# The second MLP product of a decoder layer as 2x2 block products with seven multiplications

## The chip, the cores and the metric

The kernel runs on one core of one Trainium2 chip. The metric is the device time of one execution in microseconds (us). A core has five engines with a queue each: PE (matrix products, with its weight loads shown apart as PEld), DVE (VectorE), ACT (ScalarE), POOL (GpSimd) and SP (SyncE, which here only issues DMAs). Each engine works its own queue in order and waits on semaphores for the others.

## The reference

One layer over x of 512 tokens by 1024 features, all in float32. The change touches only the last lines of it, and the residual ahead of them:

```python
merged = jax.nn.sigmoid(gate_attn) * attn + jax.nn.sigmoid(gate_conv) * conv
x = x + merged @ w_out[l]                                   # (512,1024) @ (1024,1024)

hmid = jnp.square(jax.nn.relu(rms_norm(x, norm_mlp_g[l]) @ w_ff1[l]))   # (512,1024) @ (1024,4096)
x = x + hmid @ w_ff2[l]                                     # (512,4096) @ (4096,1024)
```

Ahead of it stand the input projection, sliding-window attention over 16 heads, and a convolution of width 31 with a layer norm.

## The kernel before

**Products in three passes.** A float32 operand is split in two: a high part (a copy cast to fp32r, on ACT) and a low part (the operand minus its high part). A product takes three matmuls: high by high, high by low, low by high. `split` (lines 138 to 142) does this for a piece of weights of 128x1024: line 140 casts on ACT, line 141 subtracts on the engine it is given, POOL by default. `stationary_tiles` (from line 144) loads columns of a matrix in two DMAs of 512 KB and yields tiles for `mm_T` (lines 171 to 176), where the weights are the stationary operand. `moving_pieces` (from line 156) loads rows for `mm_M` (lines 178 to 182), where the weights are the moving operand of 512 columns. Raw weights have two buffers (tag "raw"), high and low parts three each (tags "wh", "wl").

**The order.** The code is written in the order of the computation, but a planner in the framework decides each engine's order from a cost model, with source order as priority, and gives out the buffers of a tag as they come free. Only a section at the start is ordered by hand (`manual_schedule`).

**Ahead of the MLP.** `residual` adds the w_out product to x (line 736) and squares it for the norm (738). The first 512 columns of w_out go through `moving_pieces`; the second half has its own loop (from line 750), which casts (757) and subtracts on POOL (758) in eight tiles of 128x512. `x2_norm` makes the norm of a token block with a short chain of small DVE instructions (lines 110 to 115, 133, 763) and two multiplications (767); `x2_trans` transposes it on PE and splits it into x2Th and x2Tl (192, 193).

**The MLP.** It runs in two halves (`fh`) over the 4096 hidden features. A half first makes 16 tiles of 128 hidden features by 512 tokens: 24 matmuls each (lines 174 to 176) and `ff1_evac` out of PSUM (Relu on ACT, 786; square on DVE, 787; high part on ACT, 788; low part on DVE, 789). The very first three tiles are done in two halves of 256 tokens (`EARLY`), since the last token blocks are still being normalized. Then, for each of two halves of 512 output columns, `mm_rows` multiplies them with w_ff2: 16 blocks of 128 hidden features, 4 token blocks, 3 passes (lines 180 to 182), into four PSUM banks; the sums are added to x1 on DVE (818), and in the second half stored (820). Tiles named `ps_f` in the trace are the PSUM banks of both products, `wh_f` and `wl_f` the weights' parts, `hmh` and `hml` the parts of the hidden features. Six PSUM banks (tag "mm") are shared by all of it.

Of the kernel before, what the change touches and what calls it, by code (L numbers as in the profile page):

```python
# [51 lines left out]
def tile_hybrid_block(  # L52
# [104 lines left out]
    def moving_pieces(w, r0, nk, c0, width, name, lo_eng=None):  # L157

        kk = 1024 // width
        for ch in range(nk // (2 * kk)):  # L160
            raw = wp.tile([P, 2 * kk, width], F32, name=f"rawm_{name}_{ch}", tag="raw", bufs=2)
            for j in range(2):
                r = r0 + (ch * 2 + j) * kk * P
                nc.sync.dma_start(
                    raw[:, j * kk:(j + 1) * kk, :],
                    w[r:r + kk * P, c0:c0 + width].rearrange("(k p) c -> p k c", p=P),
                )
            for j in range(2):
                yield split(raw[:, j * kk:(j + 1) * kk, :], [P, kk, width], f"{name}_{ch}_{j}", lo_eng or ge)
# [8 lines left out]
    def mm_M(ps, ah, al, wh, wl, first, last):  # L178

        pe.matmul(ps, ah, wh, start=first, stop=False)  # L180
        pe.matmul(ps, ah, wl, start=False, stop=False)  # L181
        pe.matmul(ps, al, wh, start=False, stop=last)  # L182

    def transpose_split(ps_pool, src, dst_h, dst_l, t, tag, pt="tr"):

        for half in range(2):
            tp = ps_pool.tile([P, 4, P], F32, name=f"tp_{tag}_{half}", tag=pt)
            for j in range(4):
                k = half * 4 + j
                pe.transpose(tp[:, j, :], src[half][:, j * P:(j + 1) * P], ident)  # L190
            hs = dst_h[:, half * 4:half * 4 + 4, t * P:(t + 1) * P]
            se.copy(hs, tp)  # L192
            ve.tensor_tensor(out=dst_l[:, half * 4:half * 4 + 4, t * P:(t + 1) * P],  # L193
                             in0=tp, in1=hs.bitcast(F32), op=ALU.subtract)
# [5 lines left out]
    aux = ctx.enter_context(tc.tile_pool(name="aux", bufs=2, space=PSUM))  # L200
# [70 lines left out]
    us = {}  # L271
# [421 lines left out]
    for m, (wh, wl) in enumerate(stationary_tiles(w_conv_out, 0, KD, "wc")):  # L693
        ps = psp.tile([P, S], F32, name=f"ps_co_{m}", tag="mm")
# [18 lines left out]
    x2Th = ff.tile([P, KD, S], F32R, name="x2Th")  # L713
    x2Tl = ff.tile([P, KD, S], F32R, name="x2Tl")

    def mm_rows(accs, pieces, ah, al, kk, n_major):

        n = len(pieces)
        for i in range(n - n_major):
            for j in range(kk):  # L720
                for t in range(NT):
                    k = i * kk + j
                    mm_M(accs[t], ah(k, t), al(k, t), pieces[i][0][:, j, :], pieces[i][1][:, j, :], k == 0,
                         k == n * kk - 1)
        for t in range(NT):
            for i in range(n - n_major, n):
                for j in range(kk):
# [6 lines left out]
    def residual(t, half, acc):  # L734
        cols = slice(half * S, half * S + S)
        ve.tensor_tensor(out=x1[t][:, cols], in0=x1[t][:, cols], in1=acc, op=ALU.add)
        sq = ff.tile([P, S], F32, name=f"fsq_{half}{t}", tag="tmp", bufs=5)
        se.activation(sq, x1[t][:, cols], AF.Square, accum_out=ssm[:, t, half:half + 1])
# [12 lines left out]
    pieces = []
    for i in range(NT):
        raw = wp.tile([P, 2, S], F32, name=f"raw_wout1_{i}", tag="raw", bufs=2)
        nc.sync.dma_start(raw, w_out[i * 256:(i + 1) * 256, S:D].rearrange("(k p) c -> p k c", p=P))
        for j in range(2):
            wh, wl = [ff.tile([P, S], F32R, name=f"wout1_{i}{j}{n}", tag="hm", bufs=DFF // P) for n in "hl"]
            se.copy(wh, raw[:, j, :])
            ge.tensor_tensor(out=wl, in0=raw[:, j, :], in1=wh.bitcast(F32), op=ALU.subtract)
            pieces.append((wh, wl))
# [24 lines left out]
    def ff1_evac(ps, hmh, hml, m):
        r = ff.tile([P, S], F32, name=f"r_{m}", tag="tmp", bufs=5)
        se.activation(r, ps, AF.Relu)  # L786
        ve.scalar_tensor_tensor(out=r, in0=ps, scalar=0.0, in1=r, op0=ALU.max, op1=ALU.mult)  # L787
        se.copy(hmh, r)  # L788
        ve.tensor_tensor(out=hml, in0=r, in1=hmh.bitcast(F32), op=ALU.subtract)  # L789

    NH = DFF // P // 2
    for fh in range(2):
        hmh = [ff.tile([P, S], F32R, name=f"hmh{fh}_{m}", tag="hm", bufs=2 * NH) for m in range(NH)]
        hml = [ff.tile([P, S], F32R, name=f"hml{fh}_{m}", tag="hm", bufs=2 * NH) for m in range(NH)]
        early = []
        for m, (wh, wl) in enumerate(stationary_tiles(w_ff1, fh * NH * P, NH, f"f1{fh}")):
            ps = psp.tile([P, S], F32, name=f"ps_f1{fh}_{m}", tag="mm")
            if fh == 0 and m < EARLY:
                mm_T(ps[:, 0:256], wh, wl, x2Th, x2Tl, slice(0, 256))
                early.append((ps, wh, wl))  # L800
                if m < 2:
                    x2_trans(2 + m)
                if m == EARLY - 1:
                    for i, (ps_, wh_, wl_) in enumerate(early):
                        mm_T(ps_[:, 256:512], wh_, wl_, x2Th, x2Tl, slice(256, 512))
                        ff1_evac(ps_, hmh[i], hml[i], i)
            else:
                mm_T(ps, wh, wl, x2Th, x2Tl)
                ff1_evac(ps, hmh[m], hml[m], m)
        for half in range(2):  # L810
            cols = slice(half * S, half * S + S)
            accs = [psp.tile([P, S], F32, name=f"ps_f2{fh}{half}_{t}", tag="mm") for t in range(NT)]
            pieces = list(moving_pieces(w_ff2, fh * NH * P, NH, half * S, S, f"f2{fh}{half}"))
            mm_rows(accs, pieces,
                    lambda k, t: hmh[k][:, t * P:(t + 1) * P], lambda k, t: hml[k][:, t * P:(t + 1) * P],
                    2, 2 if fh and half else 0)
            for t in range(NT):
                ve.tensor_tensor(out=x1[t][:, cols], in0=x1[t][:, cols], in1=accs[t], op=ALU.add)  # L818
                if fh:
                    nc.sync.dma_start(out[t * P:(t + 1) * P, cols], x1[t][:, cols])  # L820
# [38 lines left out]
```

## Time and profile before

| | |
|---|---|
| median of 3 runs | 827.47 us (825.0 to 829.76) |
| the profiled execution | 825.94 us, of which the span from first to last instruction is 824.1 |
| busy in the span: PE | 799.3 us (97%) |
| DVE | 464.2 us (56%) |
| ACT | 322.1 us (39%) |
| POOL | 364.5 us (44%) |
| granted clock of PE, mean | 0.996 |
| moved by DMA | 79.58 MB, mean 97 GB/s |

How to read it: a row of the profile names the line of the kernel, the engine, the operation, what it writes and reads with the shapes, the count, then busy time and mean duration of one in ns, then the idle time of the engine ahead of it and what ended most of that. "A <- B" in a list of waits says that A's engine stood still until B was done: total us, times, longest. A timeline row gives start and duration in us. Matmuls overlap, so the duration of one is longer than the distance between two.

### The profile page before, as it was taken

How to read it: one execution, taken by the hardware profiler on the slowest of the kernel's cores; microseconds unless marked ns; L12 is line 12 of the kernel's file. 1: busy time of each engine (PE TensorE's matmuls, PEld its weight loads, DVE VectorE, ACT ScalarE, POOL GpSimd, SP SyncE). 2: the span in 40 equal slices, each digit the busy share in tenths (PEclk: the TensorE clock that was granted, in tenths of full speed). 3: DMA queues.
4: the chain of work that ended last, by engine and by line, in shares of the span. 5: the costliest groups of instructions: out<-in, count | busy, mean ns of one | idle time of the engine just before them, and what ended most of it. 6: DMA issues, size and time to landing. Idle time of an engine off the chain costs nothing.

```text
span 824.1 us, 10474 instructions
## 1 busy us (share of the span) xinstructions
PE 799.3 (97%) x4056; PEld 677.2 (82%) x4056; DVE 464.2 (56%) x858; ACT 322.1 (39%) x559; POOL 364.5 (44%) x176
## 2 busy tenths in 40 slices
PE   7999898999989999998999999999999999999998
PEld 7989796978878888786888898888888888888886
DVE  5539999999999999859862833321010233320101
ACT  5452345555465544334334243442112243432110
POOL 4354436354444544452567034443444444444441
PEclk9999999999999999999999999999999999999999
DMA  7422222132131223421335022322223222222411
GB/s 267 128 79 75 89 93 82 47 102 78 54 124 54 81 73 123 151 85 51 103 127 180 25 67 89 101 103 102 103 103 103 98 81 83 97 103 103 153 51 52
DMA packets 64808, 79.58 MB, mean 97 GB/s; under 512 B 2980, under 2 KB 52180, under 8 KB 64758
## 3 DMA queue, kind: packets, MB, share of 16 engines
q1 hardware_dynamic: 64758, 78.91, 28.5%
q8 instruction: 32, 0.52, 0.3%
q14 instruction: 18, 0.15, 0.1%
HBM read 76.78 MB, written 2.12 MB: 96 GB/s over the span
## 4 chain that ended last, share of the span: by engine, by line
PE 80%; DVE 18%; DMA 1%; ACT 1%; issue 0%; SPq 0%; DVEq 0%; ACTq 0%
PE ps_f L175 7%; DVE cv L457 7%; PE ps_f L176 7%; PE ps_f L180 7%; PE ps_f L174 7%; PE ps_f L182 7%; PE ps_f L181 7%; PE ps_tc L423 2%; PE ps_tc L422 2%; PE ps_wo L180 2%; PE ps_wo L181 2%; PE ps_wo L182 2%; PE ps_tc L424 2%; PE ps_co L175 2%; PE ps_co L176 2%; PE ps_co L174 2%
## 5 line engine op out<-in xcount | busy, mean ns | idle before, releaser
L457 DVE SCALAR_TENSOR_TENSOR cv<-h,wcol,cv 128x512 f32<-128x512 f32 x240 | 167.2, 745 | 0.2
L141 POOL TENSOR_TENSOR wl_f<-raw_f,wh_f 128x1024 fp32r<-128x1024 f32 x32 | 76.7, 2401 | 113.3 <-ACT wh_f L140 113.3
L141 POOL TENSOR_TENSOR wl_f<-rawm_f,wh_f 128x1024 fp32r<-128x1024 f32 x32 | 76.5, 2389 | 98.0 <-ACT wh_f L140 98.0
L175 PE MATMUL ps_f<-x2Tl,wh_f 128*128 128x512 f32 (+1 forms) x280 | 104.1, 372 | 0.1
L174 PE MATMUL ps_f<-x2Th,wh_f 128*128 128x512 f32 (+1 forms) x280 | 103.6, 371 | 0.2 <-ACT x2Th L192 0.2
L176 PE MATMUL ps_f<-x2Th,wl_f 128*128 128x512 f32 (+1 forms) x280 | 103.8, 371 | 0.0
L180 PE MATMUL ps_f<-wh_f,hmh 128*128 128x512 f32 x256 | 99.6, 389 | 0.0
L181 PE MATMUL ps_f<-wl_f,hmh 128*128 128x512 f32 x256 | 99.6, 389 | 0.0
L182 PE MATMUL ps_f<-wh_f,hml 128*128 128x512 f32 x256 | 99.6, 389 | 0.0
L818 DVE TENSOR_TENSOR x<-x,ps_f 128x512 f32<-128x512 f32 x16 | 10.9, 688 | 156.7 <-PE ps_f L182 156.7
L140 ACT CAST wh_f<-rawm_f 128x1024 fp32r<-128x1024 f32 x32 | 33.7, 1053 | 125.8 <-PE ps_f L182 110.8
L787 DVE SCALAR_TENSOR_TENSOR r<-ps_f,r 128x512 f32<-128x512 f32 x32 | 22.1, 692 | 94.8 <-ACT r L786 94.8
L140 ACT CAST wh_f<-raw_f 128x1024 fp32r<-128x1024 f32 x32 | 33.5, 1050 | 81.6 <-PE ps_f L175 64.3
L175 PEld LDWEIGHTS ps_f<-x2Tl,wh_f 128*128 128x128 f32 x280 | 52.7, 188 | 9.3 <-DVE x2Tl L193 0.3
L174 PEld LDWEIGHTS ps_f<-x2Th,wh_f 128*128 128x128 f32 x280 | 52.6, 188 | 9.4 <-ACT x2Th L192 0.5
L176 PEld LDWEIGHTS ps_f<-x2Th,wl_f 128*128 128x128 f32 x280 | 52.7, 188 | 9.1
L525 POOL TENSOR_TENSOR s<-s,r 128x1024 f32<-128x1024 f32 (+1 forms) x16 | 26.9, 1682 | 67.9 <-DVE r L524 42.0
L182 PEld LDWEIGHTS ps_f<-wh_f,hml 128*128 128x128 f32 x256 | 48.0, 188 | 10.1
L181 PEld LDWEIGHTS ps_f<-wl_f,hmh 128*128 128x128 f32 x256 | 48.0, 188 | 10.0
L180 PEld LDWEIGHTS ps_f<-wh_f,hmh 128*128 128x128 f32 x256 | 48.0, 188 | 9.9
L789 DVE TENSOR_TENSOR hml<-r,hmh 128x512 fp32r<-128x512 f32 x32 | 34.8, 1088 | 23.0 <-ACT hmh L788 23.0
L521 ACT ACTIVATE s<-s,negm 128x257 f32<-128x257 f32 (+1 forms) x64 | 30.2, 476 | 23.5 <-DVE negm L518 14.5
(303 smaller groups left out, 1911.3 us busy)
## 6 DMA issues: line engine op xcount, KB each, us to landing
raw_f<-in_w_ff_dram SPq DMA_DIRECT2D x32, 512.0 KB, 4.3
rawm_f<-in_w_ff_dram SPq DMA_DIRECT2D x32, 512.0 KB, 3.9
x<-in_x_dram SPq DMA_DIRECT2D x8, 512.0 KB, 4.9
raw_g<-in_w_in_dram SPq DMA_DIRECT2D x8, 512.0 KB, 4.5
raw_a<-in_w_in_dram SPq DMA_DIRECT2D x8, 512.0 KB, 3.9
rawm_q<-in_w_in_dram SPq DMA_DIRECT2D x8, 512.0 KB, 3.3
raw_ta<-in_w_in_dram SPq DMA_DIRECT2D x8, 512.0 KB, 4.4
raw_tc<-in_w_in_dram SPq DMA_DIRECT2D x8, 512.0 KB, 3.4
```

What stands on the lines that cost most here:

```text
L140: hi_fn(wh, raw_ap)
L141: lo_eng.tensor_tensor(out=wl, in0=raw_ap, in1=wh.bitcast(F32), op=ALU.subtract)
L174: pe.matmul(ps, wh[:, k, :], ah[:, k, cols], start=(k == 0), stop=False)
L175: pe.matmul(ps, wh[:, k, :], al[:, k, cols], start=False, stop=False)
L176: pe.matmul(ps, wl[:, k, :], ah[:, k, cols], start=False, stop=(k == nk - 1))
L180: pe.matmul(ps, ah, wh, start=first, stop=False)
L181: pe.matmul(ps, ah, wl, start=False, stop=False)
L182: pe.matmul(ps, al, wh, start=False, stop=last)
L457: ve.scalar_tensor_tensor(out=cps[ct], in0=src, scalar=w, in1=cps[ct], op0=ALU.mult, op1=ALU.add)
L521: se.activation(s4[:, h, lo:2 * P + 1], s4[:, h, lo:2 * P + 1], AF.Exp, bias=negm[:, h:h + 1], scale=-1.0, accum_out=l4[:, h:h + 1])
L525: ge.tensor_tensor(out=s4[:, :, lo:2 * P], in0=s4[:, :, lo:2 * P], in1=r4.unsqueeze(2).to_broadcast([P, GRP, 2 * P - lo]), op=ALU.mult)
L789: ve.tensor_tensor(out=hml, in0=r, in1=hmh.bitcast(F32), op=ALU.subtract)
```

## The change

The second product is computed by a scheme of Strassen's kind (Winograd's form). Hidden features, tokens and output columns are each taken in two halves: A is the 2x2 block matrix of hmid (token halves by the even and odd blocks of hidden features), B that of w_ff2. Instead of eight block products there are seven, and fifteen sums of blocks: four of A (s1 to s4), four of B (t1 to t4), seven additions of a product's PSUM banks to x1.

- The MLP now runs in four parts of 1024 hidden features instead of two of 2048. A part makes its 8 tiles (24 matmuls each) and then seven products of 24 matmuls.
- `ff1_evac` does Relu in place in PSUM and the square on ACT. For an even tile it splits the first 256 tokens (aE); for an odd one it splits the tile (aO) and makes the four sums s1 to s4 of 256 columns on DVE, which are split as one block of 1024 columns (aS).
- w_ff2 comes in four blocks a part (b11, b12, b22, b21), each of two DMAs of 512 KB, in four buffers (tag "quarter") together with tq, which holds t3, then t2, then t4 in place. t1 is made in place in b12. b21 is loaded when b11 has been read for the last time.
- `pieces_of` splits a block in two pieces of 128x1024, the cast on ACT, the subtraction on DVE. The first piece uses the tags "wh" and "wl" (three buffers, shared with the w_ff1 tiles), the second has two buffers of its own (wh2, wl2).
- `product` accumulates into banks X, Y or Z; X and Y go on accumulating over several products, being added to x1 after each. In the very last product the order goes by token block.
- The low parts of the w_ff1 tiles are made on DVE instead of POOL (`stationary_tiles(..., ve)`).
- Around it: the rows of 4 KB (gmlp, the squares, u2, r, the sums) share one tag of five buffers; u2 is made by one instruction instead of two; the second half of w_out is cast and split in four pieces of 128x1024 instead of eight of 128x512; the scratch space of dynamic DMAs is set to 1024 bytes.

```diff
-    def mm_rows(accs, pieces, ah, al, kk, n_major):
+    def mm_rows(accs, pieces, ah, al, kk):
...
-        us[t] = [ff.tile([P, S], F32, name=f"u2_{t}{h}", tag="tmp", bufs=5) for h in range(2)]
-        for h in range(2):
-            ve.scalar_tensor_tensor(out=us[t][h], in0=x1[t][:, h * S:h * S + S], scalar=rs,
-                                    in1=gmlp[:, h * S:h * S + S], op0=ALU.mult, op1=ALU.mult)
+        us[t] = row4k(f"u2_{t}")
+        ve.scalar_tensor_tensor(out=us[t], in0=x1[t], scalar=rs, in1=gmlp, op0=ALU.mult, op1=ALU.mult)
...
+    def pieces_of(src, name):
+
+        for h in range(2):
+            shape, n = [P, 2, S], f"{name}{h}"
+            if h == 0:
+                wh = wp.tile(shape, F32R, name=f"wh_{n}", tag="wh")
+                wl = wp.tile(shape, F32R, name=f"wl_{n}", tag="wl")
+            else:
+                wh = ff.tile(shape, F32R, name=f"wh_{n}", tag="wh2", bufs=2)
+                wl = ff.tile(shape, F32R, name=f"wl_{n}", tag="wl2", bufs=2)
+            half = src[:, 2 * h:2 * h + 2, :]
+            se.copy(wh, half)
+            sub(wl, half, wh.bitcast(F32))
+            yield wh, wl
...
+        def ff1_evac(ps, m):
+            c, odd = m // 2, m % 2
+            if not odd:
+                rows_r[c] = row4k(f"r_{part}_{c}").rearrange("p (o q) -> p o q", o=2)
+            r = rows_r[c]
+            se.activation(ps, ps, AF.Relu)
+            se.activation(r[:, odd, :], ps, AF.Square)
+            if not odd:
+                hi_lo_of(aE, c, r[:, 0, 0:256])
+                return
+            hi_lo_of(aO, c, r[:, 1, :])
+            a11, a21, a12, a22 = r[:, 0, 0:256], r[:, 0, 256:S], r[:, 1, 0:256], r[:, 1, 256:S]
+            ss_t = row4k(f"ss_{part}_{c}").rearrange("p (i q) -> p i q", i=4)
+            s3, s1, s2, s4 = (ss_t[:, i, :] for i in range(4))
+            sub(s3, a11, a21)
+            ve.tensor_tensor(out=s1, in0=a21, in1=a22, op=ALU.add)
+            sub(s2, s1, a11)
+            sub(s4, a12, s2)
+            hi_lo_of(aS, c, ss_t)
...
-        for m, (wh, wl) in enumerate(stationary_tiles(w_ff1, fh * NH * P, NH, f"f1{fh}")):
+        for m, (wh, wl) in enumerate(stationary_tiles(w_ff1, part * PT * P, PT, f"f1{part}", ve)):
...
+        def load(odd, half):
+            b = quarter(f"b{odd}{half}_{part}")
+            for h in range(2):
+                nc.sync.dma_start(b[:, 2 * h:2 * h + 2, :], w2[odd][:, 2 * h:2 * h + 2, half * S:half * S + S])
+            return b
...
+        def product(a, pieces, banks, first, last, by_token=False):
+            order = [(h, t) for h in range(2) for t in range(2)]
...
+            for h, t in order:
...
+                for j in range(2):
+                    ah, al = a(t)(2 * h + j)
+                    pe.matmul(banks[t], ah, wh[:, j, :], start=(first and h + j == 0), stop=False,
+                              skip_group_check=True)
+                    pe.matmul(banks[t], ah, wl[:, j, :], start=False, stop=False, skip_group_check=True)
+                    pe.matmul(banks[t], al, wh[:, j, :], start=False, stop=(last and h + j == 2),
+                              skip_group_check=True)
...
+        b11, b12, b22 = load(0, 0), load(0, 1), load(1, 1)
+        X, Y = two_banks("x"), two_banks("y")
+        product(lambda t: a_of(aE, None, t), pieces_of(b11, f"b11_{part}"), X, True, True)
+        add(0, 0, X, False)
+        tq = quarter(f"t_{part}")
+        sub(tq, b22, b12)
+        product(S_(0), pieces_of(tq, f"t3_{part}"), Y, True, True)
+        add(1, 1, Y, False)
+        ve.tensor_tensor(out=tq, in0=tq, in1=b11, op=ALU.add)
+        product(S_(2), pieces_of(tq, f"t2_{part}"), X, False, True)
+        add(1, 0, X, False)
+        sub(b12, b12, b11)
+        b21 = load(1, 0)
+        sub(tq, b21, tq)
+        product(lambda t: a_of((aO[0][:, :, 256:S], aO[1][:, :, 256:S]), None, t),
+                pieces_of(tq, f"t4_{part}"), Y, False, True)
+        add(1, 0, Y, True)
+        product(S_(1), pieces_of(b12, f"t1_{part}"), X, False, True)
+        add(1, 1, X, True)
+        Z = two_banks("z")
+        product(lambda t: a_of(aO, None, t), pieces_of(b21, f"b21_{part}"), Z, True, True)
+        add(0, 0, Z, True)
+        product(S_(3), pieces_of(b22, f"b22_{part}"), X, False, True, part == PARTS - 1)
+        add(0, 1, X, True)
...
-    nc = _bacc.Bacc("TRN2", target_bir_lowering=False, num_devices=1)
+    nc = _bacc.Bacc("TRN2", target_bir_lowering=False, num_devices=1, dynamic_dma_scratch_size=1024)
```

More of the change, by code (lines that the diff above doesn't have):

```diff
@@ L705, in tile_hybrid_block, with row4k, quarter @@
     ff = ctx.enter_context(tc.tile_pool(name="ff", bufs=1, reuse_waits="tile"))
-    gmlp = ff.tile([P, D], F32, name="gmlp")
+    def row4k(name, dtype=F32):
+        return ff.tile([P, D], dtype, name=name, tag="row", bufs=5)
+    def quarter(name, dtype=F32):
+        return ff.tile([P, 4, S], dtype, name=name, tag="quarter", bufs=4)
+    gmlp = row4k("gmlp")
     nc.sync.dma_start(gmlp, bc(norm_mlp_g[0], P))
@@ L714, in tile_hybrid_block @@
     x2Tl = ff.tile([P, KD, S], F32R, name="x2Tl")
-    def mm_rows(accs, pieces, ah, al, kk, n_major):
+    def mm_rows(accs, pieces, ah, al, kk):
         n = len(pieces)
-        for i in range(n - n_major):
+        for i in range(n):
             for j in range(kk):
                 for t in range(NT):
[L722 to L727, printed above, removed]
                     k = i * kk + j
@@ L736, in residual @@
         ve.tensor_tensor(out=x1[t][:, cols], in0=x1[t][:, cols], in1=acc, op=ALU.add)
-        sq = ff.tile([P, S], F32, name=f"fsq_{half}{t}", tag="tmp", bufs=5)
-        se.activation(sq, x1[t][:, cols], AF.Square, accum_out=ssm[:, t, half:half + 1])
+        sq = row4k(f"fsq_{half}{t}")
+        se.activation(sq[:, 0:S], x1[t][:, cols], AF.Square, accum_out=ssm[:, t, half:half + 1])
     def m_hi(k, t):
@@ L746, in tile_hybrid_block @@
     accs = [psp.tile([P, S], F32, name=f"ps_wo0_{t}", tag="mm") for t in range(NT)]
-    mm_rows(accs, list(moving_pieces(w_out, 0, KD, 0, S, "wout0")), m_hi, m_lo, 2, 0)
+    mm_rows(accs, list(moving_pieces(w_out, 0, KD, 0, S, "wout0")), m_hi, m_lo, 2)
     for t in range(NT):
         residual(t, 0, accs[t])
-    pieces = []
+    wout_h = [quarter(f"wout1h_{i}", F32R) for i in range(2)]
+    wout_l = [quarter(f"wout1l_{i}", F32R) for i in range(2)]
     for i in range(NT):
@@ L754, in tile_hybrid_block @@
         nc.sync.dma_start(raw, w_out[i * 256:(i + 1) * 256, S:D].rearrange("(k p) c -> p k c", p=P))
[L755 to L759, printed above, removed]
+        ks = slice(2 * (i % 2), 2 * (i % 2) + 2)
+        wh, wl = wout_h[i // 2][:, ks, :], wout_l[i // 2][:, ks, :]
+        se.copy(wh, raw)
+        ge.tensor_tensor(out=wl, in0=raw, in1=wh.bitcast(F32), op=ALU.subtract)
     def x2_norm(t):
@@ L764, in x2_norm @@
         rs = rsqrt(mean_eps(ms, D, 1, f"m{t}"), 1, f"m{t}")
-        us[t] = [ff.tile([P, S], F32, name=f"u2_{t}{h}", tag="tmp", bufs=5) for h in range(2)]
-        for h in range(2):
-            ve.scalar_tensor_tensor(out=us[t][h], in0=x1[t][:, h * S:h * S + S], scalar=rs,
-                                    in1=gmlp[:, h * S:h * S + S], op0=ALU.mult, op1=ALU.mult)
+        us[t] = row4k(f"u2_{t}")
+        ve.scalar_tensor_tensor(out=us[t], in0=x1[t], scalar=rs, in1=gmlp, op0=ALU.mult, op1=ALU.mult)
     def x2_trans(t):
-        transpose_split(aux, us[t], x2Th, x2Tl, t, f"m{t}", "aux")
+        transpose_split(aux, (us[t][:, 0:S], us[t][:, S:D]), x2Th, x2Tl, t, f"m{t}", "aux")
     for t in range(NT):
@@ L775, in tile_hybrid_block @@
         for k in range(KD):
-            mm_M(acc, m_hi(k, t), m_lo(k, t), pieces[k][0], pieces[k][1], k == 0, k == KD - 1)
+            mm_M(acc, m_hi(k, t), m_lo(k, t), wout_h[k // 4][:, k % 4, :], wout_l[k // 4][:, k % 4, :],
+                 k == 0, k == KD - 1)
         residual(t, 1, acc)
@@ L781, in tile_hybrid_block, with sub @@
     x2_trans(1)
[L784 to L794, printed above, removed]
+    def sub(out, a, b):
+        ve.tensor_tensor(out=out, in0=a, in1=b, op=ALU.subtract)
@@ new lines, in tile_hybrid_block, with hi_lo_of @@
+    PARTS, PT = 4, DFF // P // 4
+    for part in range(PARTS):
+        tag = f"f{part}"
+        aS = [keep.tile([P, 4, 4, 256], F32R, name=f"aS{n}_{part}", tag="act", bufs=2) for n in "hl"]
+        aE = [ff.tile([P, 4, 256], F32R, name=f"aE{n}_{part}", tag=f"aE{n}") for n in "hl"]
+        aO = [ff.tile([P, 4, S], F32R, name=f"aO{n}_{part}", tag=f"aO{n}") for n in "hl"]
+        rows_r = {}
+        def hi_lo_of(dst, c, src):
+            se.copy(dst[0][:, c], src)
+            sub(dst[1][:, c], src, dst[0][:, c].bitcast(F32))
+        def ff1_evac(ps, m):
[17 more added lines that the diff above has]
+            hi_lo_of(aS, c, ss_t)
@@ L795, in tile_hybrid_block @@
         early = []
-        for m, (wh, wl) in enumerate(stationary_tiles(w_ff1, fh * NH * P, NH, f"f1{fh}")):
-            ps = psp.tile([P, S], F32, name=f"ps_f1{fh}_{m}", tag="mm")
-            if fh == 0 and m < EARLY:
+        for m, (wh, wl) in enumerate(stationary_tiles(w_ff1, part * PT * P, PT, f"f1{part}", ve)):
+            ps = psp.tile([P, S], F32, name=f"ps_f1{part}_{m}", tag="mm")
+            if part == 0 and m < EARLY:
                 mm_T(ps[:, 0:256], wh, wl, x2Th, x2Tl, slice(0, 256))
@@ L805, in tile_hybrid_block @@
                         mm_T(ps_[:, 256:512], wh_, wl_, x2Th, x2Tl, slice(256, 512))
-                        ff1_evac(ps_, hmh[i], hml[i], i)
+                        ff1_evac(ps_, i)
             else:
                 mm_T(ps, wh, wl, x2Th, x2Tl)
-                ff1_evac(ps, hmh[m], hml[m], m)
-        for half in range(2):
-            cols = slice(half * S, half * S + S)
[L812 to L820, printed above, removed]
+                ff1_evac(ps, m)
@@ new lines, in tile_hybrid_block, with a_of @@
+        w2 = w_ff2[part * PT * P:(part + 1) * PT * P, :].rearrange("(c two p) n -> two p c n", two=2, p=P)
+        def load(odd, half):
[3 more added lines that the diff above has]
+            return b
+        def a_of(src, i, t):
+            cols = slice(t * P, t * P + P)
+            if i is None:
+                return lambda c: (src[0][:, c, cols], src[1][:, c, cols])
+            return lambda c: (src[0][:, c, i, cols], src[1][:, c, i, cols])
@@ new lines, in product @@
+        def product(a, pieces, banks, first, last, by_token=False):
+            order = [(h, t) for h in range(2) for t in range(2)]
+            if by_token:
+                pieces, order = list(pieces), [(h, t) for t in range(2) for h in range(2)]
+            got, it = [], iter(pieces)
+            for h, t in order:
+                while len(got) <= h:
+                    got.append(next(it))
+                wh, wl = got[h]
+                for j in range(2):
[5 more added lines that the diff above has]
+                              skip_group_check=True)
@@ new lines, in add, with two_banks @@
+        def add(row, half, banks, store):
+            cols = slice(half * S, half * S + S)
+            for t in range(2):
+                n = 2 * row + t
+                ve.tensor_tensor(out=x1[n][:, cols], in0=x1[n][:, cols], in1=banks[t], op=ALU.add)
+                if store and part == PARTS - 1:
+                    nc.sync.dma_start(out[n * P:(n + 1) * P, cols], x1[n][:, cols])
+        def two_banks(name):
+            return [psp.tile([P, S], F32, name=f"ps_{name}{t}_{part}", tag="mm") for t in range(2)]
@@ new lines, in S_ @@
+        def S_(i):
+            return lambda t: a_of(aS, i, t)
+        b11, b12, b22 = load(0, 0), load(0, 1), load(1, 1)
[7 more added lines that the diff above has]
+        ve.tensor_tensor(out=tq, in0=tq, in1=b11, op=ALU.add)
```

## The prediction

> **What bounds the kernel now.** I read the page's totals first, then the busy time by stretches, then the waits inside the MLP, then the groups by shape.
>
> ```profile
> span 824.1 us, 10474 instructions
> PE 799.3 (97%) x4056; PEld 677.2 (82%) x4056; DVE 464.2 (56%) x858; ACT 322.1 (39%) x559; POOL 364.5 (44%) x176
> ```
> ```profile
> core 0: us, PE busy (x) PEld busy (x) DVE busy (x) ACT busy (x) POOL busy (x), PEclk, DMA share, GB/s
> 0.00:30.00 30.00, 25.07 (x179) 24.21 (x180) 17.81 (x33) 17.63 (x32) 11.38 (x20) 0.94 0.71 235
> 30.00:290.00 260.00, 248.89 (x1471) 217.15 (x1470) 236.04 (x512) 131.99 (x295) 124.64 (x58) 0.99 0.25 82
> 443.00:469.00 26.00, 25.76 (x122) 21.31 (x121) 17.40 (x56) 9.51 (x21) 7.19 (x4) 1.00 0.27 87
> 469.00:820.00 351.00, 350.89 (x1624) 293.54 (x1623) 74.10 (x100) 102.81 (x132) 146.05 (x61) 1.00 0.27 93
> ```
> ```profile
> PE ps_f L174 <- ACT x2Th L192: 0.2, 1, 0.2
> ```
>
> The stretch 469 to 820 is the MLP. PE is busy in 350.89 of its 351 us, and the waits of PE inside it are that single row, 0.2 us. DVE is busy in 74 us of it, ACT in 103, POOL in 146: nothing but PE sets the end there. A busy PE could still be a slow one, so the pitch matters:
>
> ```profile
> L176 PE MATMUL ps_f<-x2Th,wl_f x280: 278/389/389, 469.7 to 732.9; 128*128 128x512 f32 x116, 128*128 128x256 f32 x24
> ...
> L182 PE MATMUL ps_f<-wh_f,hml x256: 388/389/389, 559.5 to 819.9; 128*128 128x512 f32 x128
> ```
>
> The last matmul of the first product (w_ff1) starts at 732.9 and the last of the kernel at 819.9; between lie the 384 matmuls of the second half's w_ff2 product (16 k blocks, 4 token blocks, 2 column halves, 3 passes). So 87.0/384 = 0.2266 us per 128x512 matmul; the 389 ns of a row is latency, not pitch.
>
> **The matmuls removed.** Before, w_ff2 takes 32 x 4 x 2 x 3 = 768 matmuls. After, each of four parts has seven calls of product, each of 2 h x 2 t x 2 j x 3 passes = 24 matmuls of the same shape: 4 x 7 x 24 = 672. 96 fewer, -21.8 us, all of it on the path. One product lasts 24 x 0.2266 = 5.44 us; the second stage of a part lasts 38.1 us and the first (8 tiles of 24) 43.5.
>
> **What DVE gets.** Low parts of w_ff1 (32) and of the w_ff2 pieces, block sums, adds out of PSUM; POOL gets nothing in the two MLP products.
>
> ```profile
> L789 DVE TENSOR_TENSOR hml<-r,hmh 128x512 fp32r<-128x512 f32 x32 | 34.8, 1088 | 23.0 <-ACT hmh L788 23.0
> ...
> L697 DVE TENSOR_TENSOR ta<-ta,tc 128x512 f32<-128x512 f32 x8 | 19.2, 2413 | 0.2
> ...
> L818 DVE TENSOR_TENSOR x<-x,ps_f 128x512 f32<-128x512 f32 x16 | 10.9, 688 | 156.7 <-PE ps_f L182 156.7
> ...
> L314 DVE TENSOR_TENSOR vv<-ps_v,vv 128x256 fp32r<-128x256 f32 x4 | 1.7, 416 | 0.0
> ...
> L403 DVE TENSOR_TENSOR kraw<-kraw,y_k 128x1024 f32<-128x1024 f32 x1 | 1.2, 1224 | 0.0
> ```
> ```profile
> L789 DVE TENSOR_TENSOR hml<-r,hmh x32: 693/1115/1135, 485.6 to 736.1; 128x512 fp32r<-128x512 f32 x32
> ```
> ```profile
> L141 POOL TENSOR_TENSOR wl_f<-raw_f,wh_f 128x1024 fp32r<-128x1024 f32 x32 | 76.7, 2401 | 113.3 <-ACT wh_f L140 113.3
> ```
>
> hml takes 693 ns at its shortest and 1115 in the middle: two-input DVE work in SBUF is slowed while POOL runs (L697: 2413 for the same shape). With POOL idle I take 0.42 us for 256 columns, 0.69 for 512, 1.22 for 1024, and for 2048 an estimate by the same slope (0.53 per 512): 2.29.
>
> First stage, per pair of tiles: two weight lows 2.45, aE low 0.42, aO low 0.69, four block sums of 256 columns 1.69, aS low 1.22: 6.5 us in the 10.9 that PE needs. Second stage, per part: 14 piece lows 17.1, four block sums of 2048 columns (t3, t2, t1, t4) 9.2, seven adds of two 128x512 from PSUM 9.6: 35.9 us against 38.1. The part as a whole has 61.8 of 81.6. So DVE is no bound by volume, but it is 94% full in the second stage unless work moves ahead into the first. Total DVE should go from 464 to about 640.
>
> **ACT.**
>
> ```profile
> L140 ACT CAST wh_f<-rawm_f 128x1024 fp32r<-128x1024 f32 x32 | 33.7, 1053 | 125.8 <-PE ps_f L182 110.8 <-PE ps_f L175 15.1
> ...
> L788 ACT CAST hmh<-r 128x512 fp32r<-128x512 f32 x32 | 19.9, 622 | 24.3 <-DVE r L787 24.3
> L786 ACT ACTIVATE r<-ps_f 128x512 f32<-128x512 f32 x32 | 18.9, 590 | 0.0
> ...
> L258 ACT COPY qraw<-ps_q 128x256 f32<-128x256 f32 x16 | 5.9, 372 | 21.7 <-PE ps_q L182 21.7
> ```
>
> Per pair: two Relu and two Square 2.4, casts of 256, 512 and 1024 columns 0.37 + 0.62 + 1.05, two weight casts 2.1: 6.5 of 10.9. Second stage: 14 casts, 14.7 of 38.1. Not a bound; an in-place Relu in PSUM has no row, I take 0.59.
>
> **Does the order let DVE work ahead?** Written in source order, each product's operands come behind the add of the product before. The queues are not in source order:
>
> ```profile
> 444.11 2.00 ACT L140 CAST wh_f<-raw_f 128x1024 fp32r<-128x1024 f32 x2 [3.15 <-DMA raw_f<-in_w_ff_dram]
> 446.02 0.62 ACT L738 ACTIVATE fsq<-x 128x512 f32<-128x512 f32 x1
> ```
> ```profile
> 463.42 0.15 DVE L110 TENSOR_SCALAR y_m<-ms_m 128x1 int32<-128x1 int32 x1
> 463.52 0.69 DVE L193 TENSOR_TENSOR x2Tl<-tp_m,x2Th 128x512 fp32r<-128x512 f32 x1
> 464.13 0.14 DVE L111 TENSOR_SCALAR y_m<-y_m 128x1 int32<-128x1 int32 x1
> ```
>
> The cast for w_ff1 stands ahead of a Square that the source issues earlier, and a transpose's low part (x2_trans) sits inside the rsqrt of x2_norm. A planner fills a queue by what it expects to be ready; so I expect t3 and the pieces of the first two products to be made in the first stage. Two places are tight; time 0 is the start of a part's first product (b11).
>
> *The aS block.* The last tile's Relu and Square end near 1.3, the four sums at 3.1, the cast of 1024 columns at 4.2, its low at 5.4. The second product (t3) needs its fourth row block's low at 5.44 + 17 x 0.2266 = 9.3. Slack 3.9; if one 2.29 sum and one 1.22 low come first, 0.4.
>
> *The fourth product.* b21 has no buffer until b11 is read for the last time (sums t2 and t1), and tq is rewritten in place. Its DMA is issued then; the loads of w_ff2 pieces before (rawm_f) took:
>
> ```profile
> DMA to landing us min/median/max: 3.2/3.9/5.4
> ```
>
> The three slots for first halves of pieces are shared with w_ff1: t3's comes free at -5.4 (tile 6 ends), so its lows end near -3, sum t2 near -1, b21 lands by 5. The second half of t2's piece has one of two slots, free at 5.44: cast and low end at 7.7, sum t4 at 10.0, its first cast and low at 12.3; PE wants it at 16.3. Slack 4.0. If sums t2 and t1 come only after add(0,0) ends at 5.44 + 1.38, they end at 11.4, and with 4 us of landing, or 6 when two loads share the way, 15.4 to 17.4; sum, cast and low add 4.6: 20 to 22, a stall of 3.7 to 5.7 per part.
>
> So the stall's ends are 0.2 us over the whole MLP (the wait row above) and 4 x 5.7 = 23. The nearest row of a stage planned around a nearly full DVE is 30 to 290: DVE 236 of 260 (91%), PE 248.89 of 260, 4.3% lost. On 4 x 38.1 us that is 6.5. Here 76% over a part and work that can move ahead speak for less; I take half, **+3 us**.
>
> **Queues and small edits, no cost.** Waiting in DVE's queue: each add waits for PE, and the next block sum or low stands behind it; this is in the stall above. X is rewritten one product after its add starts: 1.38 against 5.44. SP still issues 32 loads of 512 KB; b21's load now waits in it for DVE, and behind it next part's w_ff1 loads, not needed for another 27 us. The eight stores stay, the last pair after the same add:
>
> ```profile
> 820.32 0.69 DVE L818 TENSOR_TENSOR x<-x,ps_f 128x512 f32<-128x512 f32 x1 [2.03 <-PE ps_f L182]
> ```
>
> That tail of 4 us remains. w_out's second half is cast and split in four pairs instead of eight tiles:
>
> ```profile
> 441.76 1.29 POOL L758 TENSOR_TENSOR wout_31l<-raw_wout,wout_31h 128x512 fp32r<-128x512 f32 x1
> ```
> ```profile
> 444.84 0.39 PE L180 MATMUL ps_wo<-wout_00h,mTh 128*128 128x512 f32 x1
> ```
>
> POOL ends its last low at 443.05; PE reaches that tile 21 matmuls after 444.84, at 449.6. A pair costs one coarser step of about 1.2 us more, covered by 6.5; without that cover +1.2. u2 in one instruction (1.22 for two of 0.69): PE idles 0.24 us of 443 to 469, so -0.2; three w_ff1 lows now beside that norm chain on DVE could delay it by one 1.22. Taken as 0, ends -0.2 and +1.2.
>
> **Sum.** The profiled execution took 825.94 us (span 824.1 and 1.84 around it): 825.9 - 21.8 + 3.0 = 807.2. The median of three runs is 827.47, 1.5 above; so **808.7**.
>
> **Rivals.** *One late operand per part (b21).* For it: the one-buffer chain above and a 94% full queue; against: two separate 4 us slacks and a planner that lost 0.2 us here so far. At the full 5.7: 805.7 + 22.8 = 828.5, no change; at half of that 817, still faster.
>
> *Long stalls also slow the clock.* The first 30 us show a clock of 0.94, 0.06 x 30 = 1.8 us lost by one start from idle; if each part's 5.7 us stall cost that again, 4 x 7.5 = 30 over 805.7: 836, slower. Against it: 1.00 all through the MLP, where nothing stalls. The Trainium skill, "TensorE: Matmul & The Clock Gate" (the HAM clock gate), says that an idle window of about 3.4 us returns PE to half rate; by that rule stalls below it would cost nothing more, and no row here shows a mid-kernel stall that long.
>
> *DVE keeps source order in the second stage (slower).* Then from a product's end: add 1.38, sum 2.29, cast 1.05, low 1.22 = 5.9 for t3 and t2; for t4 also sum t1 and the landing, 12 or more; 2.6 for each of the last three: 32 per part, 805.7 + 128 = 934. It decides as soon as a part loses over 5.45 us, that is, one product with a block sum made behind the add. Against it: the two timelines above, out of source order.
>
> **How the numbers follow.** Forecast 0.66 (804 to 814). Late operand 0.22, half below 823.3 and half within 0.5% of before (4.1 us, about what a measurement of this kernel can tell). Clock 0.04, source order 0.08, both slower. Faster 0.66 + 0.11 = 0.77, same 0.11, slower 0.12. The low end is a dense PE from the fastest run, 825.0 - 21.8, with a little added: 804; the high end 824 leaves out the slower cases and most of the late operand's upper half, about 2 in 10.
>
> **What would show it.** Right: 672 matmuls in the second stage at an unchanged pitch; PE busy in 98% or more of the MLP; waits of PE there, if any, on DVE lows or the cast of aS; POOL idle; lows of 1024 columns near 1.22, sums near 2.29; DVE near 640 us. Wrong: PE waits of several us at t3 or t4 in each part, the load of b21 landing late, a clock below 1.0 in the MLP, or DVE instructions of 1024 columns above 2 us.

## The result, and the profile after

The changed kernel takes 804.94 us (median of 4 runs, 803.17 to 808.36) against 827.98 for the kernel before on the same chips: a ratio of 0.973, 95% interval 0.9686 to 0.9774. The gain is 23.0 us; a gain of 18.8 was forecast (21.8 less 3.0, that is 808.7).

The profiled execution is the longest of the four. Its page and its busy time by stretches (columns as before):

```profile
span 806.6 us, 10416 instructions
PE 781.7 (97%) x3960; PEld 662.8 (82%) x3960; DVE 629.4 (78%) x1046; ACT 378.8 (47%) x627; POOL 210.5 (26%) x108
```
```profile
10.00:20.00 10.00, 9.46 (x53) 8.93 (x54) 7.39 (x11) 6.29 (x12) 5.70 (x2) 0.66 0.77 271
469.00:803.00 334.00, 333.01 (x1546) 278.32 (x1545) 239.97 (x299) 160.30 (x205) 0.00 (x0) 1.00 0.29 97
```

The first row is not the change's doing: between 10 and 20 us this execution was granted a clock of 0.66, for 0.83 in the kernel before's profile:

```profile
10.00:20.00 10.00, 9.06 (x62) 8.58 (x63) 7.92 (x12) 7.15 (x14) 5.72 (x2) 0.83 0.77 273
```

More of the same follows ahead of the MLP. Behind a wait of PE in the attention that both kernels have, this execution ran 3.4 us at half the clock, and the kernel before in its profile did not (the wait, the same row in both; then the stretch after it, here and before):

```profile
PE qtp L498 <- POOL qs L488: 2.2, 1, 2.2
```
```profile
99.90:103.30 3.40, 3.40 (x15) 2.82 (x14) 3.40 (x7) 1.09 (x2) 2.03 (x1) 0.50 0.13 15
```
```profile
98.90:102.30 3.40, 3.40 (x22) 2.83 (x20) 3.40 (x6) 1.16 (x3) 2.05 (x1) 1.00 0.08 15
```

This execution had three such stretches between 90 and 200 us, the kernel before had one, at 237 us. The four runs follow their mean clock: 808.4, 805.7, 804.2 and 803.2 us at 0.989, 0.992, 0.996 and 0.998. The run at 0.996, the clock of before's profiled execution, had a span of 802.4 against its 824.1. That difference is 21.7 us, the 96 matmuls at 0.2266.

The second row is the MLP, where the clock is 1.00 in both kernels. Its first matmul starts at 472.4 (468.8 before) and its last at 802.3 (819.9): 329.9 us for 351.1, 21.2 less. PE is busy in 333 of 334 us, DVE's share rose from 74 to 240 us, and POOL is silent. All waits of PE inside it:

```profile
PE ps_f L175 <- DVE x2Tl L193: 0.3, 1, 0.3
PE ps_f L174 <- ACT x2Th L192: 0.2, 1, 0.2
```

Both lie at its beginning, where the last token blocks are still being normalized. No block product ever waited: a second stage lasts 38.1 us in every part, the 168 matmuls at 0.2266. The groups of DVE by shape have the prices of the new work:

```profile
L141 DVE TENSOR_TENSOR wl_f<-raw_f,wh_f 128x1024 fp32r<-128x1024 f32 x32 | 39.1, 1224 | 57.8 <-ACT wh_f L140 56.6
L794 DVE TENSOR_TENSOR wl_b<-b,wh_b 128x1024 fp32r<-128x1024 f32 x24 | 29.4, 1223 | 22.2 <-ACT wh_b L807 22.1
L794 DVE TENSOR_TENSOR aOl<-r,aOh 128x512 fp32r<-128x512 f32 x16 | 11.0, 686 | 0.0
L794 DVE TENSOR_TENSOR t<-b,b 128x2048 f32<-128x2048 f32 x4 | 9.2, 2292 | 1.2 <-DMA b<-in_w_ff_dram 1.1
L838 DVE TENSOR_TENSOR ss<-r 128x256 f32<-128x256 f32 x16 | 6.7, 419 | 0.0
```

1224, 686, 2292 and 419 ns, where 1220, 690, 2290 and 420 had been taken. (The subtractions share one helper, so they share line 794.)

The timeline of DVE around the start of the first part's second stage (PE loads the first weights of the product of b11 at 519.4, of t3 at 524.9, of t4 at 535.7; the matmuls start 0.2 to 0.3 later):

```profile
515.27 1.22 DVE L794 TENSOR_TENSOR wl_t<-t,wh_t 128x1024 fp32r<-128x1024 f32 x1
...
516.75 2.28 DVE L912 TENSOR_TENSOR t<-t,b 128x2048 f32<-128x2048 f32 x1
...
524.78 1.23 DVE L794 TENSOR_TENSOR aSl<-ss,aSh 128x1024 fp32r<-128x1024 f32 x1 [0.17 <-ACT aSh L820]
...
527.78 2.29 DVE L794 TENSOR_TENSOR t<-b,t 128x2048 f32<-128x2048 f32 x1
529.99 1.43 DVE L894 TENSOR_TENSOR x<-x,ps_y 128x512 f32<-128x512 f32 x2
531.34 2.35 DVE L794 TENSOR_TENSOR wl_t<-t,wh_t 128x1024 fp32r<-128x1024 f32 x2
```

A piece of t3 and the sum t2 are made at 515 to 519, before even b11's product has begun. The last aS low ends at 526.0; t3's fourth row block needs it 17 matmuls after 525.1, at 529.0: slack 2.9. Sum t4 is ready at 530.1 and its first low at about 532.5; PE wants it at 536.0: slack 3.4. The other three parts show the same two slacks. There the sums t3 and t1 are made even earlier than the first stage, in the second stage of the part before.

### The profile page after: what moved, and what is told of

Its sections match the earlier page's. It is cut to its first block, busy times and chain, and to the rows that moved or that the text cites. A ratio compares the mean times of both kernels' runs of the same rounds, so it can differ in the third digit from the quotient of the medians.

```text
span 806.6 us, 10416 instructions
## 1 busy us (share of the span) xinstructions
PE 781.7 (97%) x3960; PEld 662.8 (82%) x3960; DVE 629.4 (78%) x1046; ACT 378.8 (47%) x627; POOL 210.5 (26%) x108
## 4 chain that ended last, share of the span: by engine, by line
PE 81%; DVE 14%; DMA 2%; issue 1%; POOL 1%; ACT 1%; SPq 0%; DVEq 0%; POOLq 0%; ACTq 0%
PE ps_f L175 7%; PE ps_f L176 7%; PE ps_f L174 7%; DVE cv L457 4%; PE ps_x L886 4%; PE ps_x L887 4%; PE ps_x L884 4%; PE ps_tc L422 2%; PE ps_tc L423 2%; PE ps_wo L182 2%; PE ps_wo L180 2%; PE ps_y L886 2%; PE ps_y L887 2%; PE ps_y L884 2%; PE ps_wo L181 2%; PE ps_tc L424 2%
## 5 line engine op out<-in xcount | busy, mean ns | idle before, releaser
L141 DVE TENSOR_TENSOR wl_f<-raw_f,wh_f 128x1024 fp32r<-128x1024 f32 x32 | 39.1, 1224 | 57.8 <-ACT wh_f L140 56.6
L794 DVE TENSOR_TENSOR wl_b<-b,wh_b 128x1024 fp32r<-128x1024 f32 x24 | 29.4, 1223 | 22.2 <-ACT wh_b L807 22.1
L807 ACT CAST wh_b<-b 128x1024 fp32r<-128x1024 f32 x24 | 25.3, 1055 | 40.5 <-PE ps_y L887 13.2
L807 ACT CAST wh_t<-t 128x1024 fp32r<-128x1024 f32 x24 | 24.9, 1053 | 36.8 <-DVE t L794 16.9
L180 PE MATMUL ps_q<-wh_q,uTh 128*128 128x256 f32 x128 | 36.6, 286 | 0.0
L182 PE MATMUL ps_q<-wh_q,uTl 128*128 128x256 f32 x128 | 36.3, 283 | 0.0
L181 PE MATMUL ps_q<-wl_q,uTh 128*128 128x256 f32 x128 | 36.2, 283 | 0.0
L794 DVE TENSOR_TENSOR wl_t<-t,wh_t 128x1024 fp32r<-128x1024 f32 x24 | 29.0, 1220 | 5.9 <-ACT wh_t L807 5.4
L141 POOL TENSOR_TENSOR wl_g<-raw_g,wh_g 128x1024 fp32r<-128x1024 f32 x8 | 20.0, 2511 | 31.0 <-ACT wh_g L140 31.0
L175 PE MATMUL ps_co<-sTl,wh_wc 128*128 128x512 f32 x64 | 25.0, 394 | 2.3 <-DVE sTl L682 2.3
```

The source lines that it names most:

```text
L141: lo_eng.tensor_tensor(out=wl, in0=raw_ap, in1=wh.bitcast(F32), op=ALU.subtract)
L175: pe.matmul(ps, wh[:, k, :], al[:, k, cols], start=False, stop=False)
L794: ve.tensor_tensor(out=out, in0=a, in1=b, op=ALU.subtract)
L807: se.copy(wh, half)
```

## The experiments

**Eight products instead of seven.** Is the gain the matmul count and nothing else?

```diff
-        product(lambda t: a_of(aO, None, t), pieces_of(b21, f"b21_{part}"), Z, True, True)
+        pieces8 = list(pieces_of(b21, f"b21_{part}"))
+        product(lambda t: a_of(aO, None, t), pieces8, Z, True, True)
         add(0, 0, Z, True)
+        product(lambda t: a_of(aO, None, t), pieces8, Z, True, True)
```

> In each part the product of b21 is run twice into the same banks (the second overwrites the first with the same values), so there are eight products, as many matmuls as before the change (768 instead of 672 in the second product); all DVE, ACT and DMA work stays that of the change. Theory (the gain is the matmul count at an unchanged pitch, all else is hidden): 96 x 0.2266 = +21.8 us on 805, 826 to 828, the time of before; PE without waits in the MLP. Rival (part of the gain is from elsewhere, POOL's silence or the coarser pieces): below 822.

Measured: 828.27 us, ratio to the kernel before 1.0011 (0.9993 to 1.0028).

```profile
PE 800.0 (97%) x4056; PEld 676.9 (82%) x4056; DVE 630.1 (76%) x1046; ACT 378.4 (46%) x627; POOL 210.6 (26%) x108
```
```profile
PE ps_z L884 <- DVE x L894: 0.3, 1, 0.3
```

The second fence is all that PE waits from 469 us on. With the matmuls put back, the time is that of before to a few tenths of a percent, although DVE has 166 us more work than there and POOL 154 less. The gain is the 96 matmuls; the other edits, the coarser pieces of w_out and the single u2 among them, come to nothing taken together.

**The low parts alone.** Two runs separate the move of the low parts from the block products. First the block products with POOL making w_ff1's low parts:

```diff
-        for m, (wh, wl) in enumerate(stationary_tiles(w_ff1, part * PT * P, PT, f"f1{part}", ve)):
+        for m, (wh, wl) in enumerate(stationary_tiles(w_ff1, part * PT * P, PT, f"f1{part}")):
```

> The change with the low parts of w_ff1 back on POOL; the block products stay. Theory (PE bounds, DVE has slack in the first stage): POOL runs 2.4 us per tile and DVE's two-input work in SBUF beside it takes 1.1 us instead of 0.69 per 512 columns, but DVE loses 2.45 of its 6.5 us per pair of tiles as well: no change, 803 to 808. Rival (the move to DVE was needed for the change to pay): each part loses several us at the aS block and the first sums, 810 to 825.

Measured: 806.31 us, ratio 0.9743 (0.9716 to 0.9769): not told apart from the change itself. DVE by shape:

```profile
L794 DVE TENSOR_TENSOR wl_b<-b,wh_b 128x1024 fp32r<-128x1024 f32 x24 | 35.3, 1470 | 14.2 <-ACT wh_b L807 14.2
L794 DVE TENSOR_TENSOR ss<-r 128x256 f32<-128x256 f32 x16 | 20.4, 1274 | 17.4 <-ACT r L829 17.4
L794 DVE TENSOR_TENSOR b<-b,b 128x2048 f32<-128x2048 f32 x4 | 14.0, 3496 | 0.0
```

Beside POOL the sum s3 of 256 columns takes 1274 ns on average for 419, and t1 3496 for 2286: DVE gives up 39 us of lows and loses as much in slower instructions (242 us busy in the stretch, 240 in the change), and nothing waits on either.

Then the kernel before with both products' low parts on DVE:

```diff
-        for m, (wh, wl) in enumerate(stationary_tiles(w_ff1, fh * NH * P, NH, f"f1{fh}")):
+        for m, (wh, wl) in enumerate(stationary_tiles(w_ff1, fh * NH * P, NH, f"f1{fh}", ve)):
...
-            pieces = list(moving_pieces(w_ff2, fh * NH * P, NH, half * S, S, f"f2{fh}{half}"))
+            pieces = list(moving_pieces(w_ff2, fh * NH * P, NH, half * S, S, f"f2{fh}{half}", ve))
```

> The kernel before, with the low parts of both MLP products on DVE instead of POOL and nothing else. Theory (POOL and DVE were both hidden behind PE): no change, within 0.5% of 828, with hml at 0.69 us instead of 1.09 and DVE at about 470 us busy. Rival (the move alone pays, the quieter POOL helps): under 822.

Measured: 828.45 us, ratio 1.0003 (0.9988 to 1.0018).

```profile
PE 802.1 (97%) x4056; PEld 679.4 (82%) x4056; DVE 526.5 (64%) x922; ACT 322.0 (39%) x559; POOL 211.1 (26%) x112
```
```profile
L789 DVE TENSOR_TENSOR hml<-r,hmh 128x512 fp32r<-128x512 f32 x32 | 22.1, 692 | 21.0 <-ACT hmh L788 21.0
```

hml is quick now (692 for 1088), POOL has 153 us less, and the time is the same. DVE came out at 526 us, not 470 as expected: the 64 lows (78 us) had not been added in. The move from POOL to DVE is worth nothing by itself, in either direction. (The w_ff2 lows were not put back on POOL in the changed kernel.)

**How full may DVE be?** The low part of first pieces computed twice, then that of both pieces:

```diff
             sub(wl, half, wh.bitcast(F32))
+            if h == 0:                          # left out in the second run
+                sub(wl, half, wh.bitcast(F32))
```

> The change with the low part of the first piece of each of the seven blocks computed twice: 7 x 1.22 = 8.6 us more DVE work per part, 70.4 us in 81.6, but 44.5 us for a second stage of 38.1 if that work could not move ahead. Theory (what counts is DVE's volume over a part, since the queue moves work into the first stage): under 4 us slower, 804 to 809. Rival (the second stage's 94% was the limit, so it spills): 4 x 6.4 = +26 us, about 830.

Measured: 806.18 us, ratio 0.9739 (0.9702 to 0.9776); PE has one wait of 0.2 us in the MLP, with DVE at 269 us of 334:

```profile
469.00:803.00 334.00, 332.72 (x1546) 277.77 (x1544) 268.92 (x327) 159.15 (x205) 0.00 (x0) 1.00 0.29 97
```

Free, with 44.5 us of DVE work, by its prices, belonging to a second stage of 38.1: the volume of the stage alone is not the limit. It did use up room: the slack of the last aS low falls from 2.9 us to 1.5.

> The change with the low parts of both pieces of each of the seven blocks computed twice: 17.1 us more DVE work per part, 78.9 us in 81.6 (97%), 53 in a second stage of 38.1. Theory (volume over a part counts, but the buffers limit how far ahead work can go: at most two products' pieces): it spills by part of 15 us, 5 to 12 us per part, 825 to 855. Rival A (volume alone counts): 805 to 810. Rival B (nothing moves ahead): 4 x 15 = +60, 865.

Measured: 820.0 us, ratio 0.9912 (0.9885 to 0.994): 15 us above the changed kernel, 3.8 per part, below the 5 to 12 expected. The stretch of the MLP and the first of PE's waits in it:

```profile
469.00:814.00 345.00, 337.37 (x1536) 275.25 (x1534) 297.40 (x347) 157.34 (x205) 0.00 (x0) 1.00 0.27 92
```
```profile
PE ps_z L887 <- DVE wl_b L794: 2.6, 4, 0.6
PE ps_y L887 <- DVE wl_t L794: 2.6, 4, 0.6
PE ps_x L885 <- ACT wh_t L807: 1.2, 4, 0.3
```

Waits of 0.3 to 0.6 us, four of each, one per part. The rows come to 6.4 us, less than half of what was lost. In part that is since a row counts from the end of the matmul before: across a wait of 0.64 us the starts of two matmuls lie 1.14 us apart instead of 0.2266. Of the 53 us of DVE work of the second stage, the trace of the first part has eleven instructions, 16.6 us, ahead of b11's product: both pieces of b11 and of t3 with their doubled lows, and the sums t3, t1 and t2. That is a lookahead of two products, as expected; the forecast of 5 to 12 us per part was too high all the same. So volume over a part is not the limit alone either: by the prices, 70 us in 81.6 were free and 79 cost 15 us.

**The order of DVE's queue.** Source order inside the second stage, for DVE alone:

```diff
+        with tc.manual_schedule(engines={ENG.DVE}):
             b11, b12, b22 = load(0, 0), load(0, 1), load(1, 1)
             ...
```

> The change with DVE's queue in source order inside the second stage (the hand-order section around it, for DVE alone); the work is the same. Theory (the scheme pays only because block sums and lows are made ahead of the add of the product before): a product with a block sum behind the add waits about 5.9 us, t4 12 or more, the last three 2.6 each, 32 us per part: 805 + 128 = 933; PE waits on DVE lows. Rival (DVE has room anyway, order does not matter): 805 to 812. The clock: if a stall of 3.4 us or more returns PE to a lower clock, the granted clock in the MLP falls clearly below 1.0 and the time goes above 933; if not it stays at 1.0.

Measured: 941.14 us, ratio 1.1359 (1.1325 to 1.1393). The same instructions, 136 us more. PE's waits in the MLP, then most of the second stage of the first part (513 to 585) and the first stage after it, by stretches:

```profile
PE ps_y L884 <- ACT wh_t L807: 63.7, 8, 11.9
PE ps_x L884 <- ACT wh_t L807: 16.2, 4, 4.1
PE ps_x L886 <- DVE wl_b L794: 6.3, 4, 1.9
PE ps_x L886 <- DVE wl_t L794: 4.2, 5, 1.0
PE ps_z L886 <- DVE wl_b L794: 2.6, 4, 0.6
```
```profile
513.00:585.00 72.00, 48.69 (x174) 36.04 (x173) 35.47 (x36) 18.23 (x20) 0.00 (x0) 0.83 0.17 58
585.00:629.00 44.00, 44.00 (x196) 36.42 (x195) 24.07 (x35) 21.61 (x31) 0.00 (x0) 1.00 0.31 96
```

The releaser named is ACT's cast, but the chain behind it is DVE's add and block sum, and for t4 the load of b21 too; the DVE timeline shows it for t3 and t4:

```profile
521.87 1.28 DVE L894 TENSOR_TENSOR x<-x,ps_x 128x512 f32<-128x512 f32 x2
523.06 2.28 DVE L794 TENSOR_TENSOR t<-b,b 128x2048 f32<-128x2048 f32 x1
526.46 2.36 DVE L794 TENSOR_TENSOR wl_t<-t,wh_t 128x1024 fp32r<-128x1024 f32 x2 [1.11 <-ACT wh_t L807]
...
547.75 2.29 DVE L794 TENSOR_TENSOR b<-b,b 128x2048 f32<-128x2048 f32 x1
554.91 2.29 DVE L794 TENSOR_TENSOR t<-b,t 128x2048 f32<-128x2048 f32 x1 [4.88 <-DMA b<-in_w_ff_dram]
558.31 2.36 DVE L794 TENSOR_TENSOR wl_t<-t,wh_t 128x1024 fp32r<-128x1024 f32 x2 [1.11 <-ACT wh_t L807]
```

The waits of these rows add up to 93 us. Most of the rest is slower matmuls: PE is busy for 819.9 us here, 38 more than the 781.7 of the changed kernel, with the same matmuls, and the clock is 0.83 in the second stage. PE sat 4.5, 4.1 and 11.2 us before t3, t2 and t4, and each of the three brought the clock to 0.50.

**A late b21.** One instruction of one column reads b11 after the third product's add:

```diff
         add(1, 0, X, False)
+        late = sm.tile([P, 1], F32, name=f"late_{part}", tag="ms1")
+        ve.tensor_tensor(out=late, in0=b11[:, 0, 0:1], in1=x1[3][:, 0:1], op=ALU.add)
```

> The change with one tiny DVE instruction per part that reads b11 once more after the add of the third product, so that the buffer of b21 comes free only about 17 us into the second stage instead of near its start. Theory (t4's operand chain of landing 4 to 6, sum 2.29, cast 1.05, low 1.22 is then exposed, 9 to 10 us; the fifth product, t1, can go first if the queue is filled so, which leaves about 4): 4 x 4 to 4 x 10, 821 to 845. Rival (the load lands in time in any case): 804 to 808.

Measured: 853.59 us, ratio 1.0318 (1.0291 to 1.0345): 48.7 above the changed kernel, 12.2 per part, above the range expected. The wait of PE:

```profile
PE ps_y L884 <- ACT wh_t L807: 37.7, 4, 10.0
```

and the windows around the first of the four (PE's last matmul ahead of it starts at 531.5, the next at 541.9; the column after POOL is the clock):

```profile
532.00:536.00 4.00, 0.00 (x0) 0.00 (x0) 0.78 (x2) 0.00 (x0) 0.00 (x0) 0.74 0.50 166
536.00:540.00 4.00, 0.00 (x0) 0.00 (x0) 1.49 (x1) 0.00 (x0) 0.00 (x0) 0.50 0.25 96
544.00:546.00 2.00, 2.00 (x6) 1.52 (x6) 2.00 (x3) 1.68 (x2) 0.00 (x0) 0.50 0.23 50
546.00:548.00 2.00, 2.00 (x7) 1.57 (x6) 1.68 (x2) 0.17 (x1) 0.00 (x0) 0.60 1.04 395
548.00:552.00 4.00, 4.00 (x20) 3.28 (x19) 2.76 (x4) 1.94 (x2) 0.00 (x0) 1.00 0.81 302
```

Two things were missed. t1 did not go ahead of t4. Its sum had long been made, but the casts of its pieces stood behind those of t4 in ACT's queue, and ACT waited 18.7 us for the sum t4:

```profile
540.84 1.99 ACT L807 CAST wh_t<-t 128x1024 fp32r<-128x1024 f32 x2 [18.73 <-DVE t L794]
542.74 1.99 ACT L807 CAST wh_t<-b 128x1024 fp32r<-128x1024 f32 x2
```

So the full 9.4 us on average were exposed. And the clock went to 0.50 during the wait and stayed there for 5.7 us after PE resumed: three matmuls came 0.59 to 0.67 us apart, the next nine 0.43, instead of 0.2266. That costs 3.0 us here and, over the four parts, 2.7 on average (2.1 to 3.3). 9.4 + 2.7 = 12.1 of the 12.2.

**One buffer for second pieces.**

```diff
-                wh = ff.tile(shape, F32R, name=f"wh_{n}", tag="wh2", bufs=2)
-                wl = ff.tile(shape, F32R, name=f"wl_{n}", tag="wl2", bufs=2)
+                wh = ff.tile(shape, F32R, name=f"wh_{n}", tag="wh2", bufs=1)
+                wl = ff.tile(shape, F32R, name=f"wl_{n}", tag="wl2", bufs=1)
```

> The change with one buffer instead of two for the second pieces (wh2, wl2). A second piece then can be cast only when the product before has ended, and PE wants it 2.72 us later; cast 1.05 and low 1.22 plus two hand-overs make about 2.4. Theory (slack of some 0.3 us, DVE often busy with something else at that moment): 0 to 1.5 us for each of the seven products, 810 to 840. Rival (the lookahead of two products was not needed): 804 to 808.

Measured: 821.25 us, ratio 0.9926 (0.9896 to 0.9955): 16 us, 4 per part.

```profile
PE ps_y L886 <- DVE wl_t L794: 3.4, 4, 0.9
PE ps_x L886 <- DVE wl_t L794: 3.3, 4, 0.8
PE ps_x L884 <- ACT wh_t L807: 1.5, 4, 0.4
```

The pieces of t2 and t4 arrive late, by less than 1 us each; those of t3, t1 and the b blocks do not, and why just these two was not tested. All these waits are short, and the clock stays at 1.00.

## Why the prediction was right, step by step

*The matmuls.* 96 x 0.2266 = 21.8: shown three times, by the MLP's length (21.2 less), by the equal-clock spans (21.7) and by the eighth product, which gives the time of before.

*The stall.* This term was mis-sized: +3.0, measured 0. The step that failed is the choice of the row to be nearest: the stretch 30 to 290, with DVE 91% busy and PE losing 4.3%. What PE loses there, in the changed kernel as in the other, is nearly all in four waits on the attention's chains, one on POOL (2.2 us, shown above) and three on DVE:

```profile
PE qtp L498 <- DVE attnT L554: 7.5, 3, 2.9
```

DVE is busy all through them: at 139 us ACT has the operand of attnT ready at 139.1, and DVE, at two instructions of the convolution, takes it up at 140.2. So a full DVE has a part in those waits. But they are four, each on a chain through several engines, and what they cost cannot be carried over by length of time to a stage whose operands are made ahead.

The two hand-walked slacks were the better guide, 3.9 and 4.0 forecast, 2.9 and 3.4 measured, and neither was used up. The doubled first lows show the room: 8.6 us more per part, still no wait of a product.

*DVE's prices and volume.* Each within 1%; 629 us in all for about 640.

*The order.* That sums and pieces move ahead of adds was read off two out-of-order rows of before, and it carries the whole result: in source order the same kernel is 13.6% slower than before the change. The price of that rival was 934 and 941 was measured, but that the two lie so close is luck. Stalls of 32 us per part had been summed and some 23 were found: 4.5 and 4.1 us before t3 and t2 for 5.9 (a product starts on the high part and the low need not be ready), and 0.6 to 1.5 before the last three for 2.6. The slower matmuls, about 9.5 us per part, were not in that sum and fill the gap.

*The late operand.* The chain is there, and when its slack is taken away the stall is what its steps add up to (9.4 us for 9 to 10), with the clock on top. In the change itself only one sum ever waited for a block's load, 1.1 us, and not on PE's path.

*The clock rival.* Right in kind, though it did not come into play in the MLP: each of the sixteen waits of 4.1 us or more in the source-order and late-b21 runs halved the clock. It had been priced from the start of the kernel at 1.8 us a stall; after the long waits above it was 2.1 to 3.3. The prediction found no stall that long in its rows, but its own row for 30 to 290, with a clock of 0.99, holds a stretch at half clock behind a wait of 2.3 us. The rule in the Trainium skill, "TensorE: Matmul & The Clock Gate" (the HAM clock gate), an idle window of about 3.4 us, fits in part: 4.1 us of waiting brought the half clock every time and the waits of up to 1.5 us later in the same stage did not, but waits of 1.9 to 2.9 us did it too in some cases.

*Moving low parts.* Taken as free, and it was, both ways. That leaves the seven products for eight as the only part of the change that pays.

## What to carry to other kernels

Where PE was busy without waits, trading matmuls for vector work gained matmuls times pitch, since the vector engine's volume fitted into a whole period with room to spare and its queue could run ahead. Check the period as well as the stage: here, by the prices, 86% of a period was free and 97% cost 15 us. Then look at the operands with the shortest lead, by buffers: one lost buffer cost 16 us and one late read 49, while 29 us more of busy time on the vector engine cost nothing. Count a wait of PE of 4 us or more as dearer than its length, for the clock, and one of 2 to 3 us as dearer in some executions.

## What the runs showed of the hardware

**The clock after a wait.** All sixteen waits of PE of 4.1 to 11.9 us in the source-order and late-b21 runs brought the clock to 0.50. It fell 2.1 to 5.2 us after the last matmul had ended and came back 3.4 to 6.5 us after the next began; the stretches at 0.50 behind these waits last 3.4, 6.8, 10.2 or 13.7 us. Shorter waits did it in some executions and not in others: the four waits of 2.2 to 2.9 us in the attention, the same in all ten profiles, came with such a stretch in 18 of the 40 cases, three times in the changed kernel's profile and once in that of before. In the MLP one wait of 1.9 us did it and none of up to 1.5 did. These stretches and the one at 11 us make up the difference between the mean clocks of the two profiles, 0.989 and 0.996.

**DVE beside POOL.** The slowdown goes by who starts first. With POOL on w_ff1's lows, an instruction of DVE with two inputs in SBUF that started while POOL was at a subtraction ended only after POOL had, by nearly its own length:

```profile
563.76 2.40 POOL L141 TENSOR_TENSOR wl_f<-raw_f,wh_f 128x1024 fp32r<-128x1024 f32 x1 [5.58 <-ACT wh_f L140]
...
564.83 1.60 DVE L794 TENSOR_TENSOR ss<-r 128x256 f32<-128x256 f32 x1 [3.24 <-ACT r L829]
```

So s3, of 0.42 us by itself, took 1.60, three lows of w_ff2 pieces took 3.20 for 1.22, and three of the four t1 took 3.90 for 2.29. Those that had begun before POOL's subtraction kept their time (aS lows 1.22, t3 2.29), and so did the adds out of PSUM beside it (0.69).
